# Softmax weights times values in float32: two heads at once on the array's column halves, one result bank a pair

## The chip, the cores and the metric

One core of a Trainium2 chip runs the whole program. The metric is the time of one execution on the device in microseconds (us); lower is better. Times given as the kernel's are the median of three runs; the trace is of one further, profiled execution.

The engines by the names of the rows: PE is TensorE (PEld its weight loads), DVE is VectorE, ACT is ScalarE, POOL is GpSimd, SP is SyncE, whose queue issues the transfers.

## The reference

One step of a hybrid attention layer on 512 prompt tokens and 64 new sample tokens (576 in all, D = 1024). One projection feeds two groups of eight heads of 64: "forgetting attention" (fox) and an indexed sparse attention (dsa) whose keys are chosen by a top-k over index scores. Then come the output projection, a LayerNorm, an MLP of width 4096 with squared ReLU, a second LayerNorm and a gated per-layer embedding. What the change touches is the last line of each attention, for the prompt:

```python
def fox_attend(q, k, v, cum_q, cum_k, q_pos, k_pos):
    s = jnp.einsum('bqhd,blhd->bhql', q, k, preferred_element_type=jnp.float32) * HEAD_DIM ** -0.5
    ...
    p = jax.nn.softmax(jnp.where(mask, s + decay, NEG), axis=-1)
    return jnp.einsum('bhql,blhd->bqhd', p.astype(v.dtype), v)
```

Everything is float32.

## The kernel before

The activations lie transposed, features on partitions and the 576 tokens along the free dimension. Large matrix products are made in float32r, where one matmul is one pass of TensorE over its columns: each operand is split into a high part (rounded to float32r) and a low part (the rest), and `gemm` (L278) adds three products, high x high, high x low, low x high. ScalarE makes the high parts of the weights (L182), VectorE or GpSimd the low ones (L186).

**Stages.** The index projection with the first key projection runs slice by slice as the inputs land (`split_slice`, `idx_main`, to about 29 us). Then come eight pairs of heads, four fox and four dsa. While TensorE projects k, q and v of pair p + 1, it works through the attention of pair p in ticks: `drive` runs the projection's generator and calls in nine ticks a pair. Behind pair 7 stands `wo1`, the first part of the output projection, under which the last pair's attention lies; from about 325 us on come the rest of the layer, which the change does not touch.

**A tick.** `jobs_of` lists nine jobs a pair: per head the four blocks of 128 queries, then one job for the 64 sample queries of both heads. `PLAN` says which stage of which job is called in each tick: the scores `qk` of the newest job (bank S), `addmax` (VectorE, bias and row maximum) one tick later, `exp` (ScalarE) two, `ptrans` (TensorE, transposes into bank T) and `pevac` (T to SBUF, tile PT) three, the product `pv` four, `oevac` five. `pv` and `oevac` run only for jobs with `close`: they treat two query blocks at once.

**Banks.** `psum_1` gives one bank for tag V and a ring of three for all other tags (S, T, X). A bank is given again once what reads it is done.

**The product before.** `pevac` writes PT in two parts, the high one by ScalarE (L885), the low one by VectorE (L886) from T and the high part. `v_out` transposes v (tile vtok, L757) and splits it likewise into VHL (L760, L761): for each head 128 weight columns, 64 high and 64 low. `pv` multiplies PT's two parts by them (L905): rows 0 to 63 of bank V get the product with v's high part, rows 64 to 127 the one with its low part. `oevac` copies one half out (L922) and adds the other (L923) into the tile mix. The sample job multiplies in float32, head by head, with the cached values (L896, 128 rows deep, 64 columns wide) and the new ones (L898, 64 deep), also into V. At the sample job, mix is multiplied by the row scales R (transposed reciprocal sums in a bank X; L915) and split into BH and BL (L916, L917) for the output projection.

**Order.** The program is written in the order of these calls; a scheduler places each engine's instructions by it, and each engine runs its own in the order placed. `state["rate"]` says how much of the top-k selection (`choice`) is called in per step of the projection.

**Lines that the steps touch.** L811 and L812: sample scores, each head on a corner of 64 rows by 64 columns of the array. L819 and L821: prompt scores. L64: transposes. L1129: a float32 matmul of LayerNorm, 288 columns. L704: rotation of q and k in the dsa pairs.

## Time and profile before

| | us |
|---|---|
| median of 3 runs (811.16 to 811.57) | 811.52 |
| the profiled execution | 811.2 |
| its span, first to last instruction | 809.5 |
| TensorE busy (5916 matmuls) | 791.1 |
| VectorE busy | 562.3 |
| ScalarE busy | 450.4 |
| GpSimd busy | 131.1 |

The span leaves out what lies around the program's own instructions. Busy times are unions of instructions in flight: TensorE's matmuls are pipelined, and a matmul's time in a row includes its latency, so how fast they follow each other is read from the starts. Idle time of an engine is put down to what ended it.

### The profile page before, as it was taken

Reading aid. Unit: us, or ns where it says so; the run is one execution under the profiler, and the core shown is the slowest. Engines: PE = TensorE matmul, PEld = TensorE weight load, DVE = VectorE, ACT = ScalarE, POOL = GpSimd, SP = SyncE. Lnnn points to the kernel's source line nnn. Section 1 sums busy time; section 2 is a strip of 40 time slices with the busy share of each in tenths; the row PEclk is TensorE's granted clock in tenths of the full one; section 3 lists DMA queues with packets and bytes.
Section 4 is the critical chain, followed back from the end, with each engine's and each line's share of the span. In section 5 each row is a group of like instructions: output and inputs, shape, how many; then the busy total and the mean of one; then the engine's idle time right before and its main releaser. Section 6 shows DMA issues by size and latency. Waiting matters only on the chain.

```text
span 809.5 us, 15121 instructions
## 1 busy us (share of the span) xinstructions
PE 791.1 (98%) x5916; PEld 770.7 (95%) x5916; DVE 562.3 (69%) x1156; ACT 450.4 (56%) x961; POOL 131.1 (16%) x131
## 2 busy tenths in 40 slices
PE   7999899999999999999999999999999999999997
PEld 7988898989999999999999999999999999999997
DVE  5689999974565754989855948567594765647553
ACT  5468656688888754588423626254262534626351
POOL 7202445345343000110000000000000000012200
PEclk9999999999999999999999999999999999999999
DMA  8537232345123222451312213132230413630001
GB/s 282 177 54 151 68 101 81 97 130 191 68 69 98 90 72 81 151 190 63 105 53 94 93 53 128 53 117 93 70 114 27 153 57 105 237 114 28 27 28 65
DMA packets 30215, 81.45 MB, mean 101 GB/s; under 512 B 5056, under 2 KB 8896, under 8 KB 30016
## 3 DMA queue, kind: packets, MB, share of 16 engines
q1 hardware_dynamic: 30144, 80.49, 30.6%
q8 instruction: 46, 0.75, 0.4%
q14 instruction: 25, 0.20, 0.1%
HBM read 66.38 MB, written 9.54 MB: 94 GB/s over the span
## 4 chain that ended last, share of the span: by engine, by line
PE 79%; DVE 10%; issue 5%; ACT 3%; DMA 1%; POOL 1%; SPq 0%; DVEq 0%; ACTq 0%; POOLq 0%
PE g L278 54%; PE m L278 13%; PE n L278 2%; DVE dbias L630 2%; PE V L905 2%; PE T L64 2%; DVE m L628 2%; DVE dbias L608 1%; DVE PT L886 1%; DMA iraw<-in_w_idx_dram 1%; PE S L819 1%; ACT whl L182 1%; PE S L821 1%; ACT xr L703 1%; DMA wraw<-in_w_up_dram 1%
## 5 line engine op out<-in xcount | busy, mean ns | idle before, releaser
L182 ACT CAST whl<-wraw 128x512 fp32r<-128x512 f32 (+1 forms) x226 | 134.9, 611 | 164.1 <-PE g L278 146.2
L278 PE MATMUL g<-BH,whl 128*128 128x288 f32 (+2 forms) x864 | 181.8, 297 | 0.4 <-DVE Y L1213 0.4
L278 PE MATMUL m<-AH,whl 128*128 128x288 f32 x736 | 177.8, 308 | 0.0
L186 DVE TENSOR_TENSOR whl<-wraw,whl 128x512 fp32r<-128x512 f32 (+1 forms) x192 | 130.7, 701 | 65.1 <-ACT whl L182 63.9
L278 PEld LDWEIGHTS g<-BH,whl 128*128 128x128 f32 x864 | 141.0, 188 | 2.6 <-ACT u L1322 1.1
L278 PEld LDWEIGHTS m<-AH,whl 128*128 128x128 f32 x736 | 126.5, 188 | 1.1
L278 PE MATMUL g<-BL,whl 128*128 128x288 f32 (+2 forms) x432 | 127.2, 295 | 0.0
L278 PE MATMUL m<-AL,whl 128*128 128x288 f32 x368 | 108.8, 296 | 0.0
L278 PE MATMUL g<-hidE,whl 128*128 128x288 f32 (+2 forms) x768 | 103.4, 295 | 0.0
L278 PE MATMUL g<-hidO,whl 128*128 128x288 f32 (+2 forms) x768 | 103.3, 295 | 0.0
L278 PEld LDWEIGHTS g<-hidO,whl 128*128 128x128 f32 x768 | 102.3, 188 | 0.0
L278 PEld LDWEIGHTS g<-hidE,whl 128*128 128x128 f32 x768 | 102.2, 188 | 0.1
L278 PEld LDWEIGHTS g<-BL,whl 128*128 128x128 f32 x432 | 81.3, 188 | 0.1
L278 PEld LDWEIGHTS m<-AL,whl 128*128 128x128 f32 x368 | 69.6, 189 | 0.2
L278 PE MATMUL g<-s,whl 128*128 128x288 f32 x432 | 68.3, 298 | 0.0
L1105 POOL TENSOR_TENSOR ln_s<-Y 128x576 f32<-128x576 f32 (+2 forms) x3 | 4.6, 1548 | 383.8 <-DVE Y L1388 371.2
L278 PEld LDWEIGHTS g<-s,whl 128*128 128x128 f32 x432 | 60.0, 188 | 2.3 <-DVE u L1324 1.2
L837 ACT ACTIVATE sP<-sP,st 128x128 f32<-128x128 f32 (+4 forms) x72 | 39.7, 551 | 35.4 <-DVE st L829 35.0
L186 POOL TENSOR_TENSOR whl<-wraw,whl 128x512 fp32r<-128x512 f32 x34 | 44.2, 1300 | 61.5 <-ACT whl L182 52.2
L1363 DVE SCALAR_TENSOR_TENSOR Y<-Y,g 128x576 f32<-128x576 f32 x48 | 36.0, 750 | 21.6 <-PE g L278 21.2
L886 DVE TENSOR_TENSOR PT<-T,PT 128x128 fp32r<-128x128 f32 (+1 forms) x64 | 31.1, 485 | 20.6 <-ACT PT L885 20.3
L278 PE MATMUL m<-BH,whl 128*128 128x288 f32 x192 | 43.6, 304 | 0.0
(280 smaller groups left out, 1331.6 us busy)
## 6 DMA issues: line engine op xcount, KB each, us to landing
wraw<-in_w_up_dram SPq DMA_DIRECT2D x32, 512.0 KB, 3.5
wraw<-in_w_down_dram SPq DMA_DIRECT2D x32, 512.0 KB, 3.5
wraw<-in_w_qkv_dram SPq DMA_DIRECT2D x23, 512.0 KB, 3.8
wraw<-in_w_gate_dram SPq DMA_DIRECT2D x8, 512.0 KB, 4.5
wraw<-in_w_o_dram SPq DMA_DIRECT2D x8, 384.0 KB, 3.0
out_vT_dram<-v SPq DMA_DIRECT2D x8, 288.0 KB, 2.1
Y<-in_xT_dram SPq DMA_DIRECT2D x8, 288.0 KB, 4.9
PLD<-PL SPq DMA_DIRECT2D x4, 576.0 KB, 2.8
```

The lines of the kernel that those rows point to most:

```text
L64: PE.transpose(out, in_, ident[:n, :n])
L182: ACT.copy(self.hv[h][0], src)
L186: eng.tensor_tensor(lv, src, f(hv), OP.subtract)
L278: PE.matmul(ps, W(w, kw, wc), a[:, ka, cols], start=(first and i == 0), stop=(last and i == n - 1))
L608: DVE.scalar_tensor_tensor(dst[:n, :nk], r[:n, :nk], w, dst[:n, :nk], op0=OP.mult, op1=OP.add)
L628: DVE.max(m, s)
L630: DVE.match_replace(out=s, in_to_replace=m, in_values=s, imm_value=GONE)
L703: q(lambda r=r, s=s: ACT.mul(v2(xr[r * 32:r * 32 + 32]), v[s * 32:s * 32 + 32], sc))
L837: ACT.activation(j["P"], j["P"], AF.Exp, bias=j["st"][:, 0:1], scale=-1.0, accum_out=s)
L886: DVE.tensor_tensor(t[:, 1, :n, c], v, f(t[:, 0, :n, c]), OP.subtract)
L905: PE.matmul(ps[:, c], w, j["PT"][:, x, kb, c], start=(kb == 0 and x == 0), stop=(kb == i and x == 1))
L1363: later(0, lambda y=y, m=m, s=s: DVE.scalar_tensor_tensor(y, y, s, m[:, :, :HW], op0=OP.mult, op1=OP.add))
```

## The change

For the prompt, PT and v stay float32 in one part each. `pevac` copies T once: ScalarE for the fox pairs (p < 4), VectorE for the dsa pairs. `v_out` keeps only vtok. `pv` closes with the second head of an odd block and multiplies both heads, head 0 into partitions 0 to 63 and head 1 into 64 to 127 of one bank V, which holds the four query blocks of a pair and stays until the sample job. The sample product goes into a bank X of the ring, both heads' cached values first, then both heads' new ones. `oevac` only works at the sample job: it copies R out of its bank, multiplies it with V and goes on as before. `jobs_of` puts both heads of a block next to each other. Besides, the first slice of x is loaded in two transfers and its split is shared between ScalarE and VectorE; rope32 shares the memory of mix32; the rate of the selection is 0.63 instead of 0.65.

```diff
@@ -296,7 +296,7 @@
 
     cosT = sb.tile([128, NT], F32, name="cosT")
     sinT = sb.tile([128, NT], F32, name="sinT")
-    rope32 = sb.tile([128, 5, 64], F32, name="rope32", tag="pvt", bufs=2)
+    rope32 = sb.tile([128, 5, 64], F32, name="rope32", tag="mix32")
     KcT, Vc = {}, {}
 
     def load_caches(g):
@@ -359,8 +359,10 @@
     xT = I["xT"].rearrange("p (k t) -> p k t", k=8)
     wix = I["w_idx"].rearrange("p (k c) -> p k c", k=8)
     for a, b in ((0, 1), (1, 2), (2, 4), (4, 6), (6, 8)):
-        SP.dma_start(xraw[:, a:b], xT[:, a:b])
+        SP.dma_start(xraw[:, a:b, :HW if a == 0 else NT], xT[:, a:b, :HW if a == 0 else NT])
         SP.dma_start(iraw[:, a:b], wix[:, a:b])
+        if a == 0:
+            SP.dma_start(xraw[:, 0, HW:], xT[:, 0, HW:])
         SP.dma_start(WT.raw[0][0][:, a:b], qkv[0][:, a:b])
     WT.load()
     SP.dma_start(small[:, 40:48], I["small"][:, 40:48])
@@ -388,8 +390,13 @@
     def split_slice(k):
 
         raw = WT.raw[0][0]
-        ACT.copy(AH[:, k], xraw[:, k])
-        ACT.copy(ixw(0, k), iraw[:, k])
+        if k:
+            ACT.copy(AH[:, k], xraw[:, k])
+            ACT.copy(ixw(0, k), iraw[:, k])
+        else:
+            ACT.copy(AH[:, k, :HW], xraw[:, k, :HW])
+            DVE.tensor_copy(ixw(0, k), iraw[:, k])
+            DVE.tensor_copy(AH[:, k, HW:], xraw[:, k, HW:])
         ACT.copy(w0(0, k), raw[:, k])
         POOL.tensor_tensor(ixw(1, k), iraw[:, k], f(ixw(0, k)), OP.subtract)
         DVE.tensor_tensor(AL[:, k], xraw[:, k], f(AH[:, k]), OP.subtract)
@@ -749,16 +756,10 @@
     def v_out(p):
         P, g = pair[p], p // 4
         m = tok_out(P["v32"])
-        vt = sb.tile([128, 4, 128], F32, name="vtok", tag="tok", bufs=2)
-        VHL = sb.tile([128, 4, 2, 2, 64], F32R, name="VHL", bufs=2)
+        P["vt"] = sb.tile([128, 4, 128], F32, name="vtok", bufs=2)
         SP.dma_start(O["vT"][p // 4, p % 4], P["v32"])
         P["vs"] = sb.tile([NS, 128], F32, name="vs", bufs=2)
-        P["VHL"] = VHL
-        ACT.copy(vt[:, 0:4], m.rearrange("p (b c) -> p b c", c=128))
-        tv = vt[:, 0:4].rearrange("p b (h d) -> p b h d", h=2)
-        eng = POOL if p else DVE
-        eng.tensor_copy(VHL[:, :, :, 0, :], tv)
-        eng.tensor_tensor(VHL[:, :, :, 1, :], tv, f(VHL[:, :, :, 0, :]), OP.subtract)
+        ACT.copy(P["vt"], m.rearrange("p (b c) -> p b c", c=128))
         yield 1
         yield 1
         yield 1
@@ -875,55 +876,52 @@
             ACT.copy(t[:NS, 1], ps[:NS, 128:256])
             j["PT"] = t
             return
-        i = j["i"]
-        if i % 2 == 0:
-            pt_now["t"] = sb.tile([128, 2, 2 + 2 * (i // 2), 256], F32R, name="PT", tag=f"PT{i // 2}")
+        i, hh = j["i"], j["hh"]
+        if i % 2 == 0 and hh == 0:
+            pt_now["t"] = sb.tile([128, 2, 2 + 2 * (i // 2), 256], F32, name="PT", tag=f"PT{i // 2}")
         t = j["PT"] = pt_now["t"]
-        n = i + 1
         c = slice((i % 2) * 128, (i % 2) * 128 + 128)
-        v = ps[:, :n * 128].rearrange("p (k c) -> p k c", c=128)
-        ACT.copy(t[:, 0, :n, c], v)
-        DVE.tensor_tensor(t[:, 1, :n, c], v, f(t[:, 0, :n, c]), OP.subtract)
+        v = ps[:, :(i + 1) * 128].rearrange("p (k c) -> p k c", c=128)
+        if j["p"] < 4:
+            ACT.copy(t[:, hh, :i + 1, c], v)
+        else:
+            DVE.tensor_copy(t[:, hh, :i + 1, c], v)
 
     def pv(j):
+
         P = pair[j["p"]]
-        ps = psum_1("V", 1)
-        j["O"] = ps
+        heads = [(hh, slice(hh * 64, hh * 64 + 64)) for hh in range(2)]
         if j["s"]:
+            ps = j["O"] = psum_1("X", 1)
             g, pp = divmod(j["p"], 4)
-            for hh in range(2):
-                r = slice(hh * 64, hh * 64 + 64)
+            for hh, r in heads:
                 PE.matmul(ps[r, :NS], Vc[g][:, (2 * pp + hh) * 64:(2 * pp + hh + 1) * 64], j["PT"][:, 0, r],
                           start=True, stop=False)
+            for hh, r in heads:
                 PE.matmul(ps[r, :NS], P["vs"][:, r], j["PT"][:NS, 1, r], start=False, stop=True)
             return
-        i, hh = j["i"], j["hh"]
+        i = j["i"]
+        if i == 1:
+            P["O"] = psum_1("V", 1)
         for kb in range(i + 1):
-            w = P["VHL"][:, kb, hh].rearrange("p a d -> p (a d)")
-            c = slice(0, 256) if kb < i else slice(128, 256)
-            for x in range(2):
-                PE.matmul(ps[:, c], w, j["PT"][:, x, kb, c], start=(kb == 0 and x == 0), stop=(kb == i and x == 1))
+            c = slice(0 if kb < i else 128, 256)
+            for hh, r in heads:
+                PE.matmul(P["O"][r, (i - 1) * 128 + c.start:(i + 1) * 128], P["vt"][:, kb, r], j["PT"][:, hh, kb, c],
+                          start=(kb == 0), stop=(kb == i))
 
     def oevac(j):
+        if not j["s"]:
+            return
         p = j["p"]
-        P = pair[p]
-        if "mix" not in P:
-            P["mix"] = sb.tile([128, NT], F32, name="mix32", tag="mix32")
-        mx, ps = P["mix"], j["O"]
-        if j["s"]:
-            ACT.copy(mx[:, NP:], ps[:, :NS])
-            DVE.tensor_tensor(mx[:, :NP], mx[:, :NP], j["R"], OP.mult)
-            ACT.copy(BH[:, p], mx)
-            POOL.tensor_tensor(BL[:, p], mx, f(BH[:, p]), OP.subtract)
-            return
-        hh, s = j["hh"], j["i"] // 2
-        a, b = (slice(0, 64), slice(64, 128)) if hh == 0 else (slice(64, 128), slice(0, 64))
-        t = sb.tile([128, 256], F32, name="pvt", tag="pvt", bufs=2)
-        ACT.copy(t[a], ps[b, :256])
-        DVE.tensor_tensor(mx[a, s * 256:s * 256 + 256], ps[a, :256], t[a], OP.add)
+        mx = sb.tile([128, NT], F32, name="mix32", tag="mix32")
+        ACT.copy(mx[:, NP:], j["O"][:, :NS])
+        ACT.copy(mx[:, :NP], j["R"])
+        DVE.tensor_tensor(mx[:, :NP], pair[p]["O"], mx[:, :NP], OP.mult)
+        ACT.copy(BH[:, p], mx)
+        POOL.tensor_tensor(BL[:, p], mx, f(BH[:, p]), OP.subtract)
 
     def jobs_of(p):
-        out = [dict(p=p, hh=hh, i=i, s=False, close=i % 2 == 1) for hh in range(2) for i in range(4)]
+        out = [dict(p=p, hh=hh, i=i, s=False, close=i % 2 == 1 and hh == 1) for i in range(4) for hh in range(2)]
         return out + [dict(p=p, s=True, close=True)]
 
     PLAN = (((oevac, 5), (addmax, 1), (exp, 2), (make_bias, 0), (make_bias, -1)),
@@ -949,7 +947,7 @@
                 yield 1
 
 
-    state = {"choice": None, "chosen": 0, "k": 0.0, "rate": 0.65, "logits": False}
+    state = {"choice": None, "chosen": 0, "k": 0.0, "rate": 0.63, "logits": False}
 
     PRI_C = 0
 
```

## Rows read from the trace of the kernel before

**Rows 1.** By stretch: length, busy us of PE, PEld, DVE, ACT, POOL, clock, DMA share, GB/s.

```profile
45.00:80.00 35.00, 33.66 (x237) 30.49 (x236) 31.29 (x75) 26.81 (x72) 5.55 (x6) 1.00 0.59 117
80.00:119.00 39.00, 36.28 (x281) 34.24 (x280) 37.95 (x124) 24.41 (x64) 16.15 (x15) 1.00 0.27 80
198.00:237.00 39.00, 39.00 (x303) 37.86 (x303) 21.10 (x53) 32.11 (x76) 18.89 (x15) 1.00 0.25 80
```

**Rows 2.** TensorE's timeline, sample scores: start, us from first start to last end, form, count.

```profile
85.41 0.44 PE L811 MATMUL S<-KcT,q32s 64*64 64x128 f32 x4
85.68 0.29 PE L812 MATMUL S<-k32s,q32s 64*64 64x64 f32 x4
85.89 0.40 PE L278 MATMUL m<-AH,whl 128*128 128x288 f32 x1
...
180.72 0.44 PE L811 MATMUL S<-KcT,q32s 64*64 64x128 f32 x4
...
210.50 0.44 PE L811 MATMUL S<-KcT,q32s 64*64 64x128 f32 x4
```

**Rows 3.** What TensorE waited for, 30 to 325 us: us in total, times, longest.

```profile
PE T L64 <- DVE PT L886: 2.7, 3, 1.5
PE V L896 <- DVE mix L923: 2.6, 3, 1.0
```

**Rows 4.** The chain of waits in order of time: start, us, what.

```profile
213.34 0.46 PE V L905 x4
...
220.85 0.88 PE V L905 x8
...
222.57 0.11 PE T L64
...
223.48 0.23 PE S L819
```

**Rows 5.** TensorE's timeline, a float32 product of LayerNorm.

```profile
334.68 1.14 PE L1129 MATMUL n<-ln_s,onesm 128*128 128x288 f32 x4
```

**Rows 6.** Instructions by line: count, duration min/median/max in ns, first and last start, forms.

```profile
L1129 PE MATMUL n<-ln_s,onesm x16: 377/406/432, 334.7 to 756.6; 128*128 128x288 f32 x8, 128*128 128x256 f32 x4, 128*128 128x320 f32 x4
```

**Rows 7.** TensorE's timeline, a sample product and what follows it.

```profile
101.22 0.33 PE L896 MATMUL V<-PTs,Vc 128*64 128x64 f32 x2 [0.69 <-DVE mix L923]
...
102.25 0.40 PE L278 MATMUL m<-AH,whl 128*128 128x288 f32 x1
```

**Rows 8.** Timelines of TensorE and ScalarE at two pair ends: scores, and T's copy.

```profile
131.32 0.39 PE L819 MATMUL S<-kE,qE 128*128 128x512 f32 x1
...
131.79 0.24 ACT L885 CAST PT<-T 128x128 fp32r<-128x128 f32 x1
...
162.37 0.39 PE L819 MATMUL S<-kE,qE 128*128 128x512 f32 x1
...
164.10 0.27 ACT L885 CAST PT<-T 128x128 fp32r<-128x128 f32 x1
```

**Rows 9.** VectorE's timeline at a later pair end.

```profile
223.11 0.43 DVE L923 TENSOR_TENSOR mix<-V,pvt 64x256 f32<-64x256 f32 x1 [2.09 <-ACT pvt L922]
...
224.84 0.28 DVE L886 TENSOR_TENSOR PT<-T,PT 128x128 fp32r<-128x128 f32 x1
```

**Rows 10.** The costliest groups: form, count | busy us, mean ns | idle before, releaser.

```profile
L886 DVE TENSOR_TENSOR PT<-T,PT 128x128 fp32r<-128x128 f32 (+1 forms) x64 | 31.1, 485 | 20.6 <-ACT PT L885 20.3
L923 DVE TENSOR_TENSOR mix<-V,pvt 64x256 f32<-64x256 f32 x32 | 13.5, 421 | 18.3 <-ACT pvt L922 17.8
```

**Rows 11.** Instructions by line, ScalarE's copy of v out of a bank.

```profile
L757 ACT COPY vtok<-X x8: 578/587/590, 55.2 to 273.5; 128x512 f32<-128x512 f32 x8
```

**Rows 12.** The chain of waits at the start.

```profile
3.60 0.43 SPq L362
...
4.07 6.89 DMA iraw<-in_w_idx_dram
```

**Rows 13.** The chain of waits at the end of attention.

```profile
321.29 1.45 POOL BL L917
```

## The prediction

> **What bounds the kernel now.** I read the page first, for the busy shares and the chain by line; then the busy time by stretch; then, inside the attention stretch (45 to 320 us), TensorE's timeline, its waits and the chain in order of time. By stretch [rows 1] three regimes are to be seen. From 198 us on TensorE is busy for the whole of its window, with the granted clock at full speed (2.4 GHz): there only removed TensorE time counts. From 80 to 119 us VectorE is busy for 37.95 of 39 us and TensorE for 36.28: VectorE is the late engine. From 45 to 80 us TensorE lacks 1.3 us. The repeat of the sample scores, once a pair, gives the same picture as a period [rows 2]: 85.41 to 180.72 us is three pairs, 31.8 us each, 180.72 to 210.50 is one pair, 29.8 us. Three early pairs lose 95.3 - 3 x 29.8 = 5.9 us. TensorE's waits name two losers [rows 3]: the sample product into V waits 2.6 us for the last add into mix (L923), and transposes wait 2.7 us for the subtraction that makes the low part of PT (L886). Behind 325 us nothing of the change is at work.
>
> **The change, part by part.**
>
> *Prompt weights times values, TensorE.* Now: per head one block of 4 and one of 8 matmuls, 0.46 and 0.88 us [rows 4], so 2 x 1.34 = 2.68 us a pair. After: the same number of instructions, because a float32 matmul of the program stands as two MATMULs in the trace: the two L1129 lines are four rows. These four, 288 columns wide, take 1.14 us with the last one's own 0.406 in it, so one follows another after (1.14 - 0.406) / 3 = 0.245 us [rows 5, 6]; by columns 0.218 us for 256 and 0.109 for 128. A head has one 256 and one 128 wide product for blocks 0 and 1, three and one for blocks 2 and 3: 2 x 0.327 + 2 x 0.763 = 2.18 us. All then hangs on whether the two heads, on columns 0 to 63 and 64 to 127, run side by side. The trace has no two neighbouring matmuls on different column halves with all 128 rows. Nearest: the sample scores, whose heads lie on two corners of the array (64 rows by 64 columns). Eight MATMULs, four of 128 and four of 64 columns, would take 4 x 0.109 + 4 x 0.055 = 0.66 us one behind another; the next projection starts 85.89 - 85.41 = 0.48 us after the first, with a change of tile shape at the end of it, and the first four together are done in 0.44 us, their latency included [rows 2]. They overlap. I take full overlap: 2.18 us a pair, plus a change of shape before and behind each of two blocks. Of the 0.48 us, half of 0.66 is the work of two heads side by side; 0.15 are left for the change of shape behind them. I take a little more, 0.18, for both changes of a block, so 0.36 a pair. 2.54 against 2.68: **-1.1 us** over 8 pairs. Bounds: -4.0 if the changes cost nothing (0.15 for each of the four would make it +0.8), +16.3 if the halves run one behind the other (2 x 2.18 + 0.36 - 2.68 = 2.04 a pair).
>
> *Sample product.* Now the order is cache rows, new rows, head by head; new rows are 64 rows deep, so the shape changes at each step: 101.22 to 102.25, 1.03 us, four steps of 0.26 [rows 7]. After: both heads' cache rows, then both heads' new rows: two steps if they overlap, 0.51 us. **-4.1 us** over 8 pairs. One behind another it still saves two changes of shape, some 0.2 us a pair, -1.6.
>
> *The bank of the sample product.* It leaves the single V bank for the ring of three that S, T and X share, and with L922 and L923 gone nothing has to be read out of V at that place: the 2.6 us of [rows 3] go. What is late next: the ring holds the scales R and fresh scores S, so the product takes the bank of the next pair's first transpose T and waits for its copy. At the ends of the second and third pair TensorE would come there 0.24 us after the scores start (131.56 and 162.61), and ScalarE's copy ends at 132.03 and 164.37 [rows 8]: waits of 0.5 and 1.8 us, less what the copy L922 no longer takes of ScalarE just ahead of it; I take two thirds, 1.5 us together, and none at the first pair. Ahead of the last four pairs VectorE makes the copy. Before 223.11 us it was idle for 2.09 us, and the transpose is done at 222.68 [rows 4, 9]: no wait if the copy goes then; if it stays where L886 stood it ends at 224.84 + 0.28 [rows 9], 1.4 us after the product could start (223.48 + 0.24 by the chain), four times 5.6. I take 0.3. Sum -2.6 + 1.5 + 0.3 = **-0.8 us**, bounds -2.6 to +5.3 (0.5 + 1.8 + 5.6 - 2.6).
>
> *VectorE and ScalarE.* L886 goes: 64 x 0.485 = 31.1 us [rows 10]. For the last four pairs a plain copy of the same shapes, bounded by L886's own 15.6 us, moves from ScalarE to VectorE. L923 (13.5 us) goes too, and on ScalarE the copies L922. New on ScalarE is the copy of R, 8 times, bounded by the 0.59 us of the same 128x512 copy out of X into vtok [rows 11]. GpSimd loses the split of v (VHL), which stands in none of TensorE's waits. In the early pairs VectorE loses 8 x 0.485 + 4 x 0.421 = 5.6 us: from 97% of 31.8 us (30.9) to 25.3 of 29.8, 85%. So the other stalls, 5.9 - 2.6 = 3.3 us in the three pairs and 1.3 us in the first stretch, should go in the main. I take 80%, **-3.5 us**, bounds 0 to -4.6. From 198 us on these cuts are worth nothing; if TensorE's cover there were gone, they would be worth at most their length.
>
> *Order of the jobs.* Both heads of a block now follow each other, and products close twice a pair instead of four times. V is held from the first product to the sample's evacuation, three ticks (10 us) before the next pair wants it: nothing. The rate at which the top-k selection is called falls by 3%: 24 calls a pair times 0.02, some 0.5 us less for VectorE a pair, counted at nothing; make_bias calls in what is missing, and in the late pairs VectorE has the time.
>
> *Start.* The first slice of x comes in two transfers, and one more issue, of 0.43 us and with its pause 0.47, stands ahead of all later ones on SP. The chain runs through the index weights of the third transfer, issued at 4.07 us, right behind another, and landing 6.89 us later [rows 12]; TensorE stands still before it can use them, so what the first slice gains is lost there. The landing moves by 0 to 0.47; **+0.2 us**, with -0.2 as the other end if the halves land earlier.
>
> *End of attention.* Last sample product, copy out, product with R, BH, GpSimd's BL (1.45 us), and only behind it the first up weights into freed memory [rows 13]. The copy of R puts up to 0.59 us on this; another layout of memory could take as much off. **+0.3 us**.
>
> **Sum.** -1.1 - 4.1 - 0.8 - 3.5 + 0.2 + 0.3 = -9.0 us, against the profiled execution of 811.2 us (span 809.5): 802.2. The median shown is 0.3 higher: **802.5 us**.
>
> **The rivals.** *The halves run one behind the other* (slower). For it: no row shows two column halves with the same 128 rows at once, and each half needs its own moving data from the same partitions. Against it: the corner tiles of [rows 2] write one bank at once. Prompt +16.3, sample -1.6, the rest as above: 811.5 + 16.3 - 1.6 - 3.8 = 822.4. It would be slower from the point where 45% of the second head's time is not hidden (9.0 / (17.4 + 2.5)).
> *The halves overlap, but in program order*: a head's first MATMUL starts only once the other's second has begun. Each of 16 blocks is then longer by one MATMUL, 0.218 us, each of 16 sample steps by 0.055: +4.4, 806.9. Against it: in the program all four MATMULs of the first head's sample scores stand before the second's, and the trace has all four of L811 before L812 [rows 2]. The Trainium skill, "TensorE: Matmul & The Clock Gate", Part 3 ("What overlaps and what doesn't"), has matmuls start and end strictly in program order; these rows disagree, and the measurement decides, as far as corner tiles tell of halves.
> *New waits for the old*: T's copy is late at each pair end (+5.3 for the bank) and no other stall goes: -1.1 - 4.1 + 5.3 + 0 + 0.5 = +0.6, 812.1, no change that can be told. For it: ScalarE was 0.5 and 1.8 us late in [rows 8]. Against it: VectorE's idle time in [rows 9].
>
> **How the numbers follow.** Forecast 0.61; in program order 0.12; one behind the other 0.14; new waits 0.10; a partial overlap between these 0.03. 0.2% (1.6 us) is about what a measurement of this kernel can tell from no change. Faster: 0.61, 0.12 and most of the partial case, with a little from new waits: 0.77. Same 0.08, slower 0.15. All terms at their lower ends together would make 811.5 - 4.0 - 4.1 - 2.6 - 4.6 - 0.2 - 0.5 = 795.5; since these hardly meet, the range begins at 797. It reaches to 811, over the ordered case and the milder half of new waits, and leaves out the serial one.
>
> **What would show it.** Right: the second head's matmuls start within some 20 ns of the first's, one of 256 columns every 0.22 us per half; a block of the last two query blocks lasts 1.7 us and one of the first two 0.85; the sample product 0.5 us; the period of a late pair falls from 29.8 to about 29.1 us, those of the early pairs to below 30; no wait for L923 or L886. Wrong: product blocks of 3.1 us (serial); waits of the sample product for PT's copy at each pair end; early periods still above 31 us, which would say that VectorE's split was not what held them.

## The result and the profile after

The changed kernel takes 803.86 us (median of four runs, 803.65 to 804.07) beside 811.34 us for the kernel before in the same runs (811.07 to 811.57): ratio 0.9908, interval [0.9891, 0.9925]. Forecast were 802.5 us and a range of 797 to 811. The profiled execution took 803.99 us with a span of 802.3, so 7.2 us less span than before.

The table dates the gain by landmarks of TensorE's timeline in both profiled executions: the first matmul of the first projection (L278), the starts of the sample scores of the pairs (q0 to q7), the first matmul behind attention, the end.

| landmark | before, us | after, us | after - before |
|---|---|---|---|
| first projection | 30.68 | 31.30 | +0.6 |
| q0 | 85.41 | 84.38 | -1.0 |
| q3 | 180.72 | 175.45 | -5.3 |
| q4 | 210.50 | 204.75 | -5.8 |
| q7 | 304.49 | 297.41 | -7.1 |
| behind attention | 323.42 | 316.42 | -7.0 |
| end | 809.50 | 802.28 | -7.2 |

The seven periods are 31.31, 30.47, 29.29, 29.29, 29.29, 29.29 and 34.07 us after, 32.14, 31.71, 31.46, 29.78, 29.77, 29.73 and 34.49 before: a late pair gives 0.5 us, the first three 4.2 together.

The first part of the page after, the engines' busy time:

```profile
PE 788.6 (98%) x5916; PEld 760.0 (95%) x5916; DVE 537.9 (67%) x1092; ACT 430.5 (54%) x904; POOL 118.2 (15%) x117
```

By stretch, beside [rows 1] (length, busy us of PE, PEld, DVE, ACT, POOL, granted clock, DMA share, GB/s):

```profile
45.00:80.00 35.00, 34.42 (x239) 30.92 (x240) 30.14 (x74) 25.73 (x70) 5.76 (x6) 1.00 0.61 118
80.00:119.00 39.00, 37.44 (x296) 34.03 (x293) 37.83 (x121) 23.45 (x64) 15.01 (x13) 1.00 0.30 85
119.00:158.00 39.00, 38.31 (x303) 35.01 (x302) 31.96 (x95) 26.41 (x70) 15.92 (x15) 1.00 0.32 96
...
198.00:237.00 39.00, 39.00 (x310) 36.02 (x309) 21.76 (x53) 28.63 (x65) 15.58 (x12) 1.00 0.25 78
```

VectorE lost work, and yet is as full from 80 to 119 us as before, 37.83 against 37.95 us of 39, because the top-k selection moved up. Its last operations by line, first of the kernel before, then of the changed one (columns as in [rows 6]):

```profile
L630 DVE MATCH_REPLACE8 dbiasS<-m,dbiasS x6: 332/334/346, 159.7 to 168.7; 64x192 f32<-64x192 f32 x6
...
L637 DVE MATCH_REPLACE8 dbiasS<-m,dbiasS x6: 333/334/335, 146.3 to 150.7; 64x192 f32<-64x192 f32 x6
```

The selection ends 18 us earlier. In the third period, MAX8 and MATCH_REPLACE8 took 10.9 us before and take 3.8 us after. From 80 to 119 us TensorE still lacks 1.6 us.

What TensorE waited for from 30 to 325 us, beside [rows 3] (us in total, times, longest):

```profile
PE S L820 <- DVE st L830: 1.8, 2, 1.2
```

The waits of [rows 3] for L886 and L923 are gone. In their place prompt scores (L820) wait twice for VectorE's addmax (L830), which reads the scores before them out of their bank.

TensorE's timeline after: sample scores (beside [rows 2]), such a wait, a prompt block of the last two query blocks and one of the first two (beside [rows 4]), and a sample product (beside [rows 7]). Columns: start, us from first start to last end, form, count, and the idle time before it:

```profile
84.38 0.44 PE L812 MATMUL S<-KcT,q32s 64*64 64x128 f32 x4
...
94.92 0.39 PE L820 MATMUL S<-kE,qE 128*128 128x256 f32 x1 [1.24 <-DVE st L830]
...
185.07 0.27 PE L64 MATMUL X<-ident,rows 128*128 128x128 f32 x1
185.27 0.44 PE L909 MATMUL V<-PT,vtok 128*64 128x256 f32 x2
...
185.27 1.73 PE L909 MATMUL V<-PT,vtok 128*64 128x256 f32 x16
186.94 0.40 PE L278 MATMUL m<-AH,whl 128*128 128x288 f32 x1
...
201.03 0.87 PE L909 MATMUL V<-PT,vtok 128*64 128x256 f32 x8
201.84 0.40 PE L278 MATMUL m<-AH,whl 128*128 128x288 f32 x1
...
218.35 0.34 PE L898 MATMUL X<-PTs,Vc 128*64 128x64 f32 x4
218.61 0.33 PE L901 MATMUL X<-PTs,vs 64*64 64x64 f32 x4
218.88 0.40 PE L278 MATMUL m<-AH,whl 128*128 128x288 f32 x1
```

The 16 MATMULs of the long block, 1.53 us of columns for each head, give way to the next matmul 1.67 us after the first start, the 8 of the short one after 0.81. The first two stand in one row that begins at 185.27: the second starts 7 ns behind the first, and in each half one MATMUL of 256 columns follows another after 0.216 us, the first of a block after 0.267. The sample product takes 0.53 us, two steps in place of four, and none waits at any pair end. The block starts 0.20 us behind the last transpose ahead of it.

The copies after, by line, beside [rows 10, 11] (count, duration min/median/max in ns, first and last start, forms):

```profile
L886 ACT COPY PT<-T x32: 242/418/592, 63.6 to 181.0; 128x128 f32<-128x128 f32 x8, 128x256 f32<-128x256 f32 x8, 128x384 f32<-128x384 f32 x8, 128x512 f32<-128x512 f32 x8
...
L888 DVE COPY PT<-T x32: 280/488/692, 188.7 to 304.1; 128x128 f32<-128x128 f32 x8, 128x256 f32<-128x256 f32 x8, 128x384 f32<-128x384 f32 x8, 128x512 f32<-128x512 f32 x8
...
L918 ACT COPY mix<-X x8: 585/587/590, 99.1 to 308.5; 128x512 f32<-128x512 f32 x8
```

T has one reader now, ScalarE in the first four pairs and VectorE in the last four. A plain VectorE copy takes as long as the subtraction did (488 ns in the median, 485 in the mean of [rows 10]), so what is saved is half the copies, not time of each.

### The profile page after: what moved, and what is told of

It reads as the page before. It is cut to its first block, busy times and chain, and to the rows that moved or that the text cites. A ratio compares the mean times of both kernels' runs of the same rounds, so it can differ in the third digit from the quotient of the medians.

```text
span 802.3 us, 14965 instructions
## 1 busy us (share of the span) xinstructions
PE 788.6 (98%) x5916; PEld 760.0 (95%) x5916; DVE 537.9 (67%) x1092; ACT 430.5 (54%) x904; POOL 118.2 (15%) x117
## 4 chain that ended last, share of the span: by engine, by line
PE 86%; DVE 8%; ACT 2%; DMA 1%; issue 1%; POOL 0%; SPq 0%; DVEq 0%; ACTq 0%
PE g L278 54%; PE m L278 18%; PE n L278 2%; DVE dbias L637 2%; PE V L909 2%; PE T L64 2%; DVE m L635 2%; PE S L822 1%; PE S L423 1%; PE S L820 1%; PE m L416 1%; PE m L423 1%; PE X L64 1%; DVE whl L186 1%; DVE dbias L615 1%
## 5 line engine op out<-in xcount | busy, mean ns | idle before, releaser
L278 PE MATMUL g<-BH,whl 128*128 128x288 f32 (+2 forms) x864 | 181.8, 298 | 0.1
L278 PE MATMUL m<-AH,whl 128*128 128x288 f32 x736 | 178.3, 309 | 0.0
L278 PEld LDWEIGHTS g<-BH,whl 128*128 128x128 f32 x864 | 141.2, 188 | 2.3 <-ACT u L1320 1.2
L278 PEld LDWEIGHTS m<-AH,whl 128*128 128x128 f32 x736 | 126.4, 188 | 3.7 <-issue 2.2
L278 PE MATMUL g<-BL,whl 128*128 128x288 f32 (+2 forms) x432 | 127.4, 295 | 0.0
L278 PE MATMUL m<-AL,whl 128*128 128x288 f32 x368 | 109.2, 297 | 0.0
L278 PE MATMUL g<-hidE,whl 128*128 128x288 f32 (+2 forms) x768 | 103.4, 295 | 0.0
L278 PE MATMUL g<-hidO,whl 128*128 128x288 f32 (+2 forms) x768 | 103.3, 295 | 0.0
L278 PEld LDWEIGHTS g<-hidO,whl 128*128 128x128 f32 x768 | 102.3, 188 | 0.0
L278 PEld LDWEIGHTS g<-hidE,whl 128*128 128x128 f32 x768 | 102.2, 188 | 0.1
L278 PEld LDWEIGHTS g<-BL,whl 128*128 128x128 f32 x432 | 81.4, 188 | 0.1
L278 PEld LDWEIGHTS m<-AL,whl 128*128 128x128 f32 x368 | 69.6, 189 | 0.5
L278 PE MATMUL g<-s,whl 128*128 128x288 f32 x432 | 68.5, 298 | 0.0
L278 PEld LDWEIGHTS g<-s,whl 128*128 128x128 f32 x432 | 60.1, 188 | 2.2 <-DVE u L1322 1.1
L278 PE MATMUL m<-BH,whl 128*128 128x288 f32 x192 | 43.5, 304 | 0.0
L278 PEld LDWEIGHTS m<-BH,whl 128*128 128x128 f32 x192 | 32.1, 188 | 0.8 <-issue 0.5
```

Source lines behind the costliest of these rows:

```text
L278: PE.matmul(ps, W(w, kw, wc), a[:, ka, cols], start=(first and i == 0), stop=(last and i == n - 1))
```

## The experiments

My theory behind the result: the halves run side by side, so the prompt product comes out even and the sample product halves; the waits at the pair ends go because T has one reader; what is left in the early pairs is VectorE's load. The rivals: overlap depends on the order of issue; the bank of the sample product did it alone; the start paid for a part; and what is left in the early pairs is something other than load. Medians are given beside those of the kernel before from the same chip.

**Head after head in the prompt product.** From the changed kernel, loops exchanged:

```diff
-        for kb in range(i + 1):
-            c = slice(0 if kb < i else 128, 256)
-            for hh, r in heads:
+        for hh, r in heads:
+            for kb in range(i + 1):
+                c = slice(0 if kb < i else 128, 256)
```

> The changed kernel, with the prompt products of a block in another order: all of head 0's, then all of head 1's, where the change alternates. Theory A, each column half is a stream of its own whatever the program order (as the sample scores show for corner tiles): blocks stay at 0.81 and 1.66 us, the time within 1 us of 803.9. Theory B, the halves overlap only where neighbours in the program lie on different halves and matmuls start in program order: head 1 waits for head 0, a block of blocks 2 and 3 lasts near 3 us and one of blocks 0 and 1 near 1.4, some 2 us more a pair, 817 to 820.

Measured: 810.26 us (809.55 to 812.1), before 811.15, ratio 0.9993 [0.9984, 1.0002]. That lies between the two expectations: neither free nor serial. TensorE's timeline of this kernel, the same long block:

```profile
186.90 2.65 PE L909 MATMUL V<-PT,vtok 128*64 128x256 f32 x16
189.48 0.40 PE L278 MATMUL m<-AH,whl 128*128 128x288 f32 x1
```

The block lasts 2.58 us in place of 1.67, and its single MATMULs say why (start of each, us):

```
head 0  186.904 187.171 187.387 187.602 187.818 188.034 188.250 188.359
head 1  187.824 188.091 188.307 188.522 188.738 188.954 189.170 189.279
```

Head 1's first starts 6 ns after head 0's fifth: once only three of head 0's are still waiting in front of it. So one MATMUL can start ahead of others that stand before it in the program. From there both run side by side. The late period is 30.21 us, 0.92 above that of the changed kernel, which is four MATMULs of 256 columns (4 x 0.216 = 0.86). The short block, with four MATMULs a head, loses nothing that can be told (0.81 us).

**Two by two.** If a MATMUL can pass three that wait for the other half, groups of four MATMULs a head must overlap fully. From the changed kernel:

```diff
-        for kb in range(i + 1):
-            c = slice(0 if kb < i else 128, 256)
+        for k0 in range(0, i + 1, 2):
             for hh, r in heads:
+                for kb in (k0, k0 + 1):
+                    c = slice(0 if kb < i else 128, 256)
```

> The changed kernel with the heads alternating after two products (four MATMULs) instead of one. In the run with a whole head after the other, head 1's first of eight started when head 0's fifth did, and blocks of four ran side by side. Theory C, a matmul can start past at most three that wait for the other half, so groups of four still overlap in full: within 0.7 us of 803.9, late periods 29.3 us. Theory B, starts are in program order and only neighbours overlap: a long block has one pair of neighbours on different halves at each of three seams, near 2.8 us, late periods 30.4 us or more, 810 to 813.

Measured: 804.37 us (803.87 to 804.55), before 810.82, ratio 0.9920 [0.9905, 0.9935]. The late period is 29.35 us, 0.06 above the changed kernel's, and the long block takes 1.72 us. Four in a row cost nearly nothing, eight cost 0.92. The Trainium skill, "TensorE: Matmul & The Clock Gate", Part 3 ("What overlaps and what doesn't"), has matmuls start in program order; these two kernels disagree where neighbours lie on different halves of the array, and the measurement decides.

**The old order of the sample product.** From the changed kernel, the second loop over the heads taken out, so that each head's two steps follow each other:

```diff
                           start=True, stop=False)
-            for hh, r in heads:
                 PE.matmul(ps[r, :NS], P["vs"][:, r], j["PT"][:NS, 1, r], start=False, stop=True)
```

> The changed kernel with the sample product head by head again: cached rows, new rows of head 0, then those of head 1, so the tile shape changes at each step. Theory A, the sample order is worth what the timeline shows (1.03 against 0.53 us a pair): 803.9 + 8 x 0.5 = 807.9, between 807 and 808.5. Rival, the order is worth less, because the time comes back in the early pairs where TensorE waits anyway: 803.9 + 5 x 0.5 = 806.4 or less.

Measured: 807.12 us (806.62 to 807.28), before 811.15, ratio 0.9950 [0.9935, 0.9965]: 0.42% of 811 us, 3.4 us, more than the changed kernel. Its timeline at a later pair end:

```profile
219.41 0.33 PE L898 MATMUL X<-PTs,Vc 128*64 128x64 f32 x2
219.67 0.32 PE L900 MATMUL X<-PTs,vs 64*64 64x64 f32 x2
219.93 0.33 PE L898 MATMUL X<-PTs,Vc 128*64 128x64 f32 x2
220.19 0.33 PE L900 MATMUL X<-PTs,vs 64*64 64x64 f32 x2
220.44 0.40 PE L278 MATMUL m<-AH,whl 128*128 128x288 f32 x1
```

Four steps of 0.26 us, 1.03 in all, as in [rows 7]. The late periods are 0.50 us longer each, as theory A has it; the second, which holds a wait anyway, is not (30.48 against 30.47 us), as the rival has it, so fewer than 4 us are lost in all. The term of the sample product is shown, and so is that the order brings it. That the alternating shape is what keeps the two heads apart in the old order is likely, but no run separates it from the order.

**The bank alone.** From the kernel before, only the sample product's bank moved:

```diff
-        ps = psum_1("V", 1)
+        ps = psum_1("X" if j["s"] else "V", 1)
```

> The kernel before with one edit: the sample product goes into a bank X of the ring instead of the V bank. Theory A, the wait for the last add into mix is 2.6 us of lost TensorE time, and little takes its place: 811.3 - 2 = 809.3, between 808.5 and 810.5. Rival, the product now waits for the copy of the next pair's T at each pair end (up to 1.8 us each, behind both ScalarE and VectorE): 811 to 816, no gain or slower.

Measured: 816.61 us (815.91 to 817.42), before 811.15, ratio 1.0066 [1.0049, 1.0083]: slower by 5.5 us, and above even the rival's range. What TensorE waited for from 30 to 325 us:

```profile
PE X L896 <- DVE PT L886: 5.9, 4, 2.0
PE T L64 <- DVE PT L886: 2.5, 3, 1.5
```

TensorE's timeline around one of these waits:

```profile
133.58 0.33 PE L896 MATMUL X<-PTs,Vc 128*64 128x64 f32 x2 [1.29 <-DVE PT L886]
...
135.73 0.44 PE L278 MATMUL m<-AL,whl 128*128 128x288 f32 x1
135.97 0.68 PE L278 MATMUL m<-AH,whl 128*128 128x288 f32 x2
```

The sample product waits for T's second reader, L886, four times and up to 2 us: the wait of which the prediction's upper bound for the bank is made.

In the changed kernel it does not wait, but not because T has one reader less. At the first three pair ends T's copy is done only behind the start of the sample product (100.65, 130.72 and 159.95 us against 99.99, 130.46 and 159.75), so the product isn't written where T stands. What is done just ahead of it is ScalarE's new copy of the scales R out of their bank (L918): 0.26 to 0.66 us ahead at the first six pair ends. Lines of both engines' timelines at the second pair end:

```profile
129.21 0.59 ACT L918 COPY mix<-X 128x512 f32<-128x512 f32 x1
...
130.46 0.34 PE L898 MATMUL X<-PTs,Vc 128*64 128x64 f32 x4
...
130.47 0.25 ACT L886 COPY PT<-T 128x128 f32<-128x128 f32 x1
```

A single sample product waits in the run with VectorE's load given back (below), and that wait ends with the same copy of R, which stands at L921 there:

```profile
162.84 0.34 PE L901 MATMUL X<-PTs,Vc 128*64 128x64 f32 x4 [0.89 <-ACT mix L921]
```

So by these rows the product gets the bank of R, which the change empties early with a copy, where before the multiplication L915 read it. A kernel without that copy alone was not run.

**The start.** First on the kernel before, then undone on the changed one:

```diff
-        SP.dma_start(xraw[:, a:b], xT[:, a:b])
+        SP.dma_start(xraw[:, a:b, :HW if a == 0 else NT], xT[:, a:b, :HW if a == 0 else NT])
         SP.dma_start(iraw[:, a:b], wix[:, a:b])
+        if a == 0:
+            SP.dma_start(xraw[:, 0, HW:], xT[:, 0, HW:])
...
+            ACT.copy(AH[:, k, :HW], xraw[:, k, :HW])
+            DVE.tensor_copy(ixw(0, k), iraw[:, k])
+            DVE.tensor_copy(AH[:, k, HW:], xraw[:, k, HW:])
```

> The kernel before with the change's start alone: the first slice of x in two transfers and its split shared between ScalarE and VectorE. Theory A, the changed kernel is 0.6 us late at its first projection because of these lines (an issue more ahead of the chain, and the clock granted in full at 11.4 instead of 9.2 us): 811.3 + 0.6, between 811.5 and 812.2. Rival, the late clock belongs to that one profiled execution: within 0.2 us of 811.3.

> The changed kernel with the start of before (first slice of x in one transfer, split on ScalarE). Theory A, the change's start costs 0.6 us: 803.9 - 0.6, between 802.9 and 803.5. Rival, the start is neutral in the time: 803.7 to 804.1.

Measured: 811.28 us with the new start on the kernel before (810.58 to 811.98), before 811.15, ratio 1.0001 [0.9992, 1.0010]; 803.22 us with the old start on the changed kernel (803.0 to 803.48), before 811.01, ratio 0.9904 [0.9889, 0.9919] beside 0.9908. The second time lies in theory A's range, but the kernel before was 0.3 us faster there too, and the ratios differ by 0.0004, well inside their intervals. In the profiled executions the first projection starts between 30.21 and 31.30 us with the new start and between 30.27 and 30.68 us with the old one. The start does nothing that can be told, and the 0.6 us of the table above belongs to that one execution.

**One block less.** From the changed kernel, both prompt blocks of a pair put into one, so that the array changes shape twice less a pair:

```diff
-        out = [dict(p=p, hh=hh, i=i, s=False, close=i % 2 == 1 and hh == 1) for i in range(4) for hh in range(2)]
+        out = [dict(p=p, hh=hh, i=i, s=False, close=i == 3 and hh == 1) for i in range(4) for hh in range(2)]
...
+        for i in (1, 3):
+            for kb in range(i + 1):
```

> The changed kernel with both prompt blocks of a pair in one: the products of all four query blocks run when the last is transposed, so a pair has one change of tile shape into and one out of the column halves instead of two. Theory A, the changes of shape are what made the prompt product dearer than forecast, some 0.3 us for a block's two: 803.9 - 8 x 0.3 = 801.5, between 801 and 802.5. Rival, the time lies in the passes themselves: 803.5 to 804.2.

Measured: 801.66 us (801.45 to 802.26), before 811.01, ratio 0.9887 [0.9870, 0.9903]. The late period falls from 29.29 to 28.96 us. Its timeline:

```profile
183.01 0.60 PE L64 MATMUL X<-ident,rows 128*128 128x128 f32 x4
183.53 2.38 PE L909 MATMUL V<-PT,vtok 128*64 128x256 f32 x24
185.85 0.40 PE L278 MATMUL m<-AH,whl 128*128 128x288 f32 x1
```

2.32 us for all 24 MATMULs, against 1.67 + 0.81 = 2.48 for two blocks: 0.15 of the 0.33 us. Another 0.09 is the way into the short block, which starts 0.33 us behind 512 columns of scores, where another matmul starts 0.23 behind them. The last 0.09 lies in the projection: its first matmul behind a block is followed after 0.24 us, where 0.13 is usual. So a block pays 0.33 us for changing shape and back, where the prediction had 0.18. The first two periods fall too, to 30.50 and 30.05 us.

With the old start as well:

> The changed kernel with both prompt blocks of a pair in one and with the start of before. If the two effects add (2.2 us for the block, and 0.2 to 0.6 for the start): 801.1 to 801.6. If the start was only a matter of when the clock is granted: 801.4 to 801.9.

Measured: 801.48 us (801.42 to 802.2), before 810.82, ratio 0.9888 [0.9871, 0.9904]: the same as the one before it. These two are the fastest kernels here. With a lower rate of calling the top-k selection on top (0.60 in place of 0.63):

> The same, and the top-k selection called at a rate of 0.60 instead of 0.63. Theory A, VectorE's load still holds the first two pairs: 24 calls a pair times 0.03 are 0.7 us less of it in each, so 0.5 to 1.5 us under the run without it. Rival, the selection comes late for the first dsa pair, or the load no longer decides: no gain, or up to 2 us slower.

Measured: 802.67 us (801.98 to 803.02), before 810.82, ratio 0.9899 [0.9884, 0.9913]: no gain, but 1.2 us more than at the rate of 0.63. Its first two periods, 31.36 and 30.57 us, are 0.9 and 0.5 us longer than at 0.63 (30.50 and 30.07), though less of the selection is called in: theory A, that VectorE's load holds these pairs, finds nothing for it here.

**Less for VectorE ahead of attention.** From the changed kernel, more weight splits given to GpSimd:

```diff
-            U[kind, p] = WT.add(qkv[p * 3 + x], pool_l=(p * 3 + x > 6))
+            U[kind, p] = WT.add(qkv[p * 3 + x], pool_l=(p * 3 + x > 3))
```

> The changed kernel with the low parts of the weights made by GpSimd from the fifth unit on instead of the eighth: VectorE loses six subtractions of 0.7 us in the first two pairs, GpSimd gains six of 1.3 us. Theory A, VectorE's load still holds the first two pairs (their periods are 31.3 and 30.5 us against 29.3): 803.9 - 1.5, between 802 and 803.4. Rival, another wait holds them, or GpSimd's parts come late: 803.5 to 806.

Measured: 812.87 us (812.48 to 813.77), before 811.01, ratio 1.0024 [1.0013, 1.0036]: 10 us are lost ahead of the first pair (q0 at 94.71 us), in part at the lower clock (granted 0.50 from 77.8 to 84.6 us). GpSimd's timeline of this kernel:

```profile
54.92 1.27 POOL L186 TENSOR_TENSOR whl<-wraw,whl 128x512 fp32r<-128x512 f32 x1 [2.53 <-ACT whl L182]
69.39 0.41 POOL L583 TENSOR_SCALAR_AFFINE_SELECT biasS<-biasS 64x256 f32<-64x256 f32 x1 [13.19 <-DMA biasS<-cS]
...
70.68 3.09 POOL L186 TENSOR_TENSOR whl<-wraw,whl 128x512 fp32r<-128x512 f32 x2
```

The splits on which TensorE now depends stand on GpSimd behind L583, which waits 13.19 us for a transfer. This kernel says little on VectorE's load, since another queue took over; behind q0 its first two periods are 30.57 and 30.47 us, beside 31.31 and 30.47 of the changed kernel.

**VectorE's load given back.** From the changed kernel, behind ScalarE's copy of T a subtraction of the old L886's shape, whose result nobody reads:

```diff
             ACT.copy(t[:, hh, :i + 1, c], v)
+            junk = sb.tile([128, 4, 128], F32, name="junk")[:, :i + 1]
+            x = t[:, hh, :i + 1, c]
+            DVE.tensor_tensor(junk, x, x, OP.subtract)
```

> The changed kernel plus one idle subtraction on VectorE behind each copy of T in the four fox pairs, of the shape of the removed one (32 instructions, some 15 us), from and to SBUF, so that no bank is held longer. Theory A, the early pairs were slow because VectorE was full: their periods go back to 31 us and more, 803.9 + 2 to 4, between 805.5 and 808. Theory B, it was the chain through two engines that held T's bank, not the load: within 0.7 us of 803.9.

Measured: 807.80 us (807.49 to 808.14), before 811.01, ratio 0.9961 [0.9946, 0.9975]: 4 us of the gain go, 2.9 of them in the third pair (32.23 us in place of 29.29) and 0.9 between the first projection and q0 (53.95 us in place of 53.08). The first two periods stay at 31.30 and 30.52 us. So theory A's time came out, but not by the pairs that it named.

The same load, but the subtraction reads bank T, which so has its second reader again:

```diff
+            DVE.tensor_tensor(junk, v, t[:, hh, :i + 1, c], OP.subtract)
```

> The changed kernel plus the idle subtraction on VectorE in the four fox pairs, this time reading T's bank as the removed one did, so the same load as in the run with the SBUF subtraction (807.8) and the bank held for a second engine. Theory A, the ring of three banks is what the removal of that second reader frees: the sample product waits again for T at the ends of the first three pairs, 0.5 to 2 us each, 810 to 814. Rival, only the load counts: within 1 us of 807.8.

Measured: 803.11 us (802.4 to 804.13), before 810.82, ratio 0.9906 [0.9891, 0.9921]: as fast as the changed kernel. Both theories fell. The third period, from q2 to q3, of the kernel with the load alone (columns as above):

```profile
146.59:178.82 32.23, 30.59 (x233) 27.38 (x232) 26.95 (x72) 24.36 (x58) 13.60 (x11) 1.00 0.28 93
```

The third period of the kernel that reads T as well:

```profile
144.56:173.85 29.29, 29.29 (x232) 27.23 (x232) 24.86 (x70) 23.25 (x56) 12.18 (x11) 1.00 0.31 101
```

VectorE is busy for 84% of the one and 85% of the other; TensorE stands idle for 1.6 us in the one and not at all in the other. Both have the selection back in that period, 11.6 and 10.9 us of it, where the changed kernel has 3.8. The first two periods of the latter are 28.89 and 29.29 us, without a stall; of the 3.6 us that this gives, 2.0 are lost ahead of q0 (86.37 us). Nor does the second reader hold the sample product: at the first pair end it ends at 100.70 us, 1.1 us behind the product's start. In the third pair of the kernel with the load alone, TensorE waits for the addmax (0.50 us at 156.82) and for R's copy (0.89 us at 162.84). So neither the load nor the second reader alone makes TensorE wait. What differs, to be seen at the first pair, is the order on VectorE. First the changed kernel's VectorE, ahead of TensorE's wait at 94.92 us:

```profile
93.26 0.43 DVE L635 MAX8 m<-dbias 128x8 f32<-128x256 f32 x1
...
93.80 0.41 DVE L637 MATCH_REPLACE8 dbias<-m,dbias 128x256 f32<-128x256 f32 x1
94.25 0.43 DVE L635 MAX8 m<-dbias 128x8 f32<-128x256 f32 x1
94.59 0.27 DVE L830 CUSTOM_DVE_ANT_0 sP<-S,causal 128x128 f32<-128x128 f32 x1
```

Then the kernel that reads T twice, at the same job of the same pair:

```profile
92.38 0.41 DVE L637 MATCH_REPLACE8 dbias<-m,dbias 128x256 f32<-128x256 f32 x1
92.70 0.68 DVE L888 TENSOR_TENSOR junk<-T,PT 128x512 f32<-128x512 f32 x1
93.30 0.28 DVE L830 CUSTOM_DVE_ANT_0 sP<-S,causal 128x128 f32<-128x128 f32 x1
```

In the changed kernel the scores are done at 90.9 us; from then on seven MAX8 and MATCH_REPLACE8 of the top-k selection (L635, L637) run back to back, and the addmax, 0.27 us of work, comes at 94.59. TensorE, which wants that bank for the next scores, stands still for 1.24 us. In the other kernel the scores are done at 92.4, the addmax starts at 93.30, and TensorE doesn't stop. The kernel before shows the same queue ahead of L886, for which TensorE waits up to 1.5 us [rows 3]. ScalarE's high part is done at 92.84 us; VectorE's timeline behind that goes on with the selection, whose last operation stands here ahead of L886:

```profile
94.22 0.41 DVE L630 MATCH_REPLACE8 dbias<-m,dbias 128x256 f32<-128x256 f32 x1
94.66 0.69 DVE L886 TENSOR_TENSOR PT<-T,PT 128x512 fp32r<-128x512 f32 x1
95.27 0.41 DVE L829 CUSTOM_DVE_ANT_0 sP<-S,causal 128x256 f32<-128x256 f32 x1
```

The rows show the short operation behind seven of the top-k's where TensorE stalls, and 0.9 us behind the scores where it doesn't. Why the order differs between these kernels stays open, and a kernel that moves only the addmax ahead of the selection was not tried, so that the order is the cause is argued from these rows and not shown. By an estimate it could bring the first two periods to 29.29 us, 31.31 + 30.47 - 2 x 29.29 = 3.2 us.

## Why the prediction was right, and where it wasn't

Sign and likeliest case were right, and the size nearly: -9.0 forecast, -7.2 in the profiled executions, -7.5 in the medians. The terms, each by its own rows, add up to -7.3; the bank's and VectorE's parts of the early periods are told apart by the lengths of the waits:

| term | forecast, us | measured, us | from |
|---|---|---|---|
| prompt product | -1.1 | +0.2 | blocks 1.67 + 0.80, ways in |
| sample product | -4.1 | -4.0 | 1.03 to 0.53 a pair |
| its bank | -0.8 | -2.6 | waits gone, no new ones |
| VectorE, ScalarE | -3.5 | -1.3 | first stretch and early periods |
| start | +0.2 | +0.6 | one execution; nothing by the runs |
| end of attention | +0.3 | 0.0 | 3.30 us from sample product to the next stage, 3.29 after |
| rest of the layer | 0 | -0.2 | last two landmarks |

The sum is nearer than its terms: the bank came out 1.8 us better than forecast, VectorE's share 2.2 and the prompt product 1.3 us worse. That these offset each other is luck.

**Prompt product.** The overlap is right to the figure: a second head 7 ns behind the first, 0.216 us a MATMUL, blocks of 1.67 and 0.81 us where 1.7 and 0.85 were to show it. The mis-sized term is the change of shape. The way out of the block was read from the sample scores, the way in counted as nearly nothing. But the way in costs 0.20 us behind transposes, where the next matmul otherwise starts 0.03 behind one, and 0.33 against 0.23 behind scores. So a pair takes 2.47 + 0.17 + 0.09 = 2.73 us. The prediction's 2.68 us for the kernel before is read from two of a pair's four blocks; by their starts the four of a late pair take 0.40, 0.87, 0.46 and 0.97, so 2.71. That is +0.2 over eight pairs; the prediction's own bound (0.15 for each change, +0.8) held. The kernel with one block less shows the price by itself: 0.33 us.

**Sample product.** Right, and shown by undoing its order alone.

**The bank.** The step that failed is "the product takes the bank of the next pair's first transpose T and waits for its copy". That is so with the bank alone on the kernel before, 5.9 us in four waits, but not in the changed kernel, where the product starts ahead of the end of T's copy at the first three pair ends and, by the rows above, gets the bank of R. The prediction counted the new copy of R as work for ScalarE, not as what empties a bank in time. So the full 2.6 us came off by a path that it didn't have.

**VectorE and ScalarE.** The step that failed is the mechanism, "VectorE is the late engine", by which 80% of the other stalls were to go with its load. Of 3.3 us of other stalls in the three early pairs 0.2 went: the three periods lost 4.24 us, of which 3 x 0.48 are the two products and 2.6 the bank's. The first stretch lost 1.65 us, of which 0.53 only moved, since the short block of both heads (0.81) stands there in place of one head's two blocks (1.34); the tail got as much back. So 1.1 + 0.2. In the first stretch the load does count: given back, it takes 0.9 of the 1.1 us again. The third pair lost its stalls in a kernel where most of the selection has left that pair, 3.8 us in place of 10.9; but the kernel that reads T twice has 10.9 us of it there and no stall either. The prediction named the sign of its own error: early periods still above 31 us. One is, one is at 30.47. A busy share close to one says that an engine could be late, not that its load is the reason: the two kernels with the extra subtraction have the same share in the third pair and differ by the whole stall.

**The rivals.** One behind the other: refuted by the long block. Program order: refuted as put, since a MATMUL passes up to three others, and half right, since it doesn't pass more; with the loops the other way round this rival's mechanism takes the whole gain. New waits for the old: true for the bank alone, not for the change as a whole; but the place of an old wait was taken in another way, from L886 to L830, both late behind the same top-k operations.

**What stays open.** How the schedule decides where the addmax stands among the top-k operations, and so why the first two pairs kept a stall. Neither the copy of R nor the rate of 0.63 was undone alone.

## What to carry to other kernels

Two narrow float32 products on different column halves are worth issuing alternately, a few matmuls at a time, and worth gathering into one long run, because a block of another shape costs more (0.33 us) than a step of a small product (0.26). Before work is taken off an engine that looks full, look at the order of its queue at the very wait: a short operation that frees a bank can stall TensorE when it stands behind a row of others; of two kernels here with the same share one lost 2.9 us in a pair and the other nothing. And moving a product into a ring of banks pays only if the bank that it gets has been read out by then: here an early copy of R empties it. An experiment that gives load back should be made in two ways, as these two show.

## What the runs showed of the hardware

- Two float32 streams with all 128 rows and different column halves run fully side by side, 5 to 8 ns apart, each with a 256-column MATMUL every 0.216 us behind a first step of 0.267.
- A MATMUL for one half starts ahead of up to three that wait for the other half: in the kernel with head after head the second head began with the first head's fifth of eight, and with groups of four next to nothing was lost (0.06 us a late period).
- A block of another shape between full-array matmuls cost 0.33 us a time, 0.09 of it on the way in behind scores, 0.15 in the blocks and 0.09 in the projection behind. Behind transposes the way in costs 0.17 above the usual step.
- In the kernel with the bank alone moved, TensorE stood still for 1.29 us at 133.58 us and was busy for 1.71 of the 3 us from 131 to 134; from 135.4 to 138.8 us the granted clock was 0.52, the lower level of 1.2 GHz, and matmuls of 288 columns came 0.24 us apart instead of 0.13. The wait was paid a second time behind it. The same followed the wait of 2.01 us at 167.60 us (granted 0.50 from 169.65 us for 3.4 us), but not the wait of 1.61 us at 101.77 us, where the clock stayed at full speed.

The last point's stretches, from the kernel with the bank alone moved (columns as above):

```profile
131.00:134.00 3.00, 1.71 (x13) 1.20 (x11) 2.87 (x7) 1.50 (x6) 2.92 (x4) 1.00 0.51 131
135.40:138.80 3.40, 3.40 (x18) 3.38 (x17) 2.25 (x5) 1.38 (x4) 1.43 (x1) 0.52 0.08 20
...
169.65:173.05 3.40, 3.40 (x17) 3.39 (x16) 1.61 (x8) 2.21 (x5) 2.66 (x2) 0.50 0.27 98
```
